# Stage B of a two-layer attention kernel: alternating scale and add on GpSimd, a PSUM copy in the normalisation, and split key buffers

## The chip, the cores and the metric

The kernel is one program on one NeuronCore of a Trainium2 chip. The metric is the device time of one launch in microseconds. The kernel before takes 1666.49 us as the median of three runs (1663.46 to 1671.07). The work is laid out over the engines of the core: TensorE (PE in the profile, with its weight loads shown apart as PEld), VectorE (DVE), ScalarE (ACT), GpSimd (POOL), and SyncE (SP), whose queue issues most of the DMAs.

## The reference

The reference is a two-layer transformer block on 1024 image tokens (`x`) and 256 context tokens (`ctx`), 1024 wide, everything in float32. The even layer projects into two attentions, A (a windowed one) and B, and a gate; the odd layer has two other attentions. The change lies in attention B, the differential attention with 4 heads: each head has two queries and two keys of 64 features and one value of 128.

```python
def _diff_attend(q, k, v, lam):
    s = jnp.einsum('bqhte,bkhte->bhtqk', q, k).astype(jnp.float32) * (q.shape[-1] ** -0.5)
    p = jax.nn.softmax(s, axis=-1)
    a = (p[:, :, 0] - lam * p[:, :, 1]).astype(v.dtype)
    return jnp.einsum('bhqk,bkhe->bqhe', a, v)
...
    yb = _sweep_query_blocks(lambda n, qn: _diff_attend(qn, kb_all, vb_all, lam), qb)
    yb = rmsnorm(yb, b_subln_g) * (1.0 - lam_init)
    y = jnp.concatenate([ya.reshape(B, S, -1), yb.reshape(B, S, -1)], axis=-1) * jax.nn.silu(g)
    x = x + gate * (y @ w_out)
```

The latent queries see 1280 keys (1024 latent and 256 context ones); the context queries see the 256 context keys alone.

## The kernel before

The kernel runs in stages, one after the other: start, e1, A, **B**, outE, then the odd layer (o1, D, M, outO). Numbers are held as a high and a low part, so one product costs two or three matmuls. Stage B is `b_scores`, `b_values`, `b_norm` and a filler, `gates`.

- **Units.** There are 20 units: 4 heads, and in each head five pairs of query blocks of 128, in the order (8,9), which are the context queries, then (0,1), (2,3), (4,5), (6,7). A unit runs its scores, then its values; after unit (8,9), (2,3) and (6,7) a normalisation follows, 12 in all, 8 of four blocks and 4 of two.
- **Scores** (`b_scores`, lines 881 to 932). For each of the two blocks and of the two halves `t`, three chunks of keys are multiplied into PSUM (`sps`, line 909), VectorE moves them to an SBUF tile `sB_t` with the running minimum (line 407), ScalarE takes the exponential (line 917). There are 7 such tiles (`S_BUFS_B`). The keys of a head are one tile `kb` of both halves, and there is one buffer for it (`K_BUFS_B` = 1), so the load for the next head (line 886) can go only when the last score of this head has been multiplied.
- **Mixing.** Half 1 is scaled by `cB` and added to half 0. For the second block VectorE does it in one instruction (line 930); for the first, GpSimd scales five pieces of 256 columns (line 927) and then adds five pieces (line 928, in the helper at line 218).
- **Values** (`b_values`). In steps of two key blocks, four transposes fill one of two PSUM tiles `tps` (`T_PS` = 2, line 958), ScalarE casts the high part `phb` (line 221), VectorE subtracts for the low part `plb` (line 214), and the products go to `pvps` (lines 418 to 420).
- **Normalisation** (`b_norm`). The result is copied out of `pvps` (line 980), transposed into a `tps` tile (line 984), squared and summed by ScalarE out of that tile (line 988); VectorE makes the reciprocal root (lines 990 to 992, 188 to 201) and multiplies out of the same `tps` tile (line 994); the product is transposed back (line 1000) and written out. The `tps` tile is held from line 984 to line 994.
- **Filler.** `gates` projects the gate in eight parts out of the layer's input `hE` (lines 304 to 306), and behind the last of them loads and splits the output weights `woE`, in memory that `hE` has left.

`pipeline` emits these streams in a fixed interleaving; the framework's scheduler then sorts each engine's instructions by its own estimate of when they are ready, and each engine runs its list strictly in that order.

Of the kernel before, what the change touches and what calls it, by code (L numbers as in the profile page):

```python
# [9 lines left out]
F32 = mybir.dt.float32  # L10
F32R = mybir.dt.float32r
BF16 = mybir.dt.bfloat16
I32 = mybir.dt.int32
AF = mybir.ActivationFunctionType
# [17 lines left out]
SM_COND, SM_GE, SM_GO, SM_SUB, SM_SINK, SM_LAM, SM_QG, SM_BE, SM_BO = 0, 16, 24, 32, 33, 41, 297, 300, 316  # L32
SM_N = 332
FILL_A, FILL_B, FILL_D, FILL_M = 5.0, 5.0, 4.3, 5.0
S_BUFS_A, S_BUFS_B, S_BUFS_D, S_BUFS_M, K_BUFS_B, Q_BUFS_B = 11, 7, 12, 6, 1, 3
PH_A, PH_D, PH_M = 3, 3, 4
FILL_O1, HL_BUFS, FILL_E1 = 3.0, 3, 2.3
FILL_Q, FILL_LAT, EMIT_C, RAW_O, RAW_3 = 9.0, 1.5, 1, 1, 2
# [58 lines left out]
def body(nc, tc, I, out, dbg=None):  # L97
# [82 lines left out]
    def f32(ap):  # L180
        return ap.bitcast(F32)
# [694 lines left out]
    with ExitStack() as st:  # L876
        bp = pool(st, "attB", 2, side="left")
        fp = pool(st, "fillB", 2, side="left")
        KB, VBt, OB = {}, {}, {}

        def b_scores(hd, grp, res):
            ctx_q = grp[0] == 8
            q = G if hd == 0 and grp[0] in POOL_Q else SY
            if hd not in KB:
                KB[hd] = bp.tile([P, 2, T], F32R, tag="K", name="kb", bufs=K_BUFS_B)
                q.dma_start(f32(KB[hd]), QK[9 + hd])
            K = KB[hd]
            Q = bp.tile([P, 2, 2, 256], F32R, tag="Q", name="qb", bufs=Q_BUFS_B)
            for half in range(2):
                for t in range(2):  # L890
                    q.dma_start(f32(Q[half * 64:(half + 1) * 64, t]),
                                QK[5 + hd][t * 64:(t + 1) * 64, :, grp[0] * P:grp[0] * P + 256])
            ks = [(S, L)] if ctx_q else list(CHUNKS)
            ncol = sum(n for _, n in ks)
            if grp[0] % 4 == 0:
                OB[hd, "s"] = tiny.tile([P, 4], F32, tag="s0g", name="s0g")
            s0g = OB[hd, "s"]
            Ps = []
            for i in range(2):
                E_ = []  # L900
                ssum = tiny.tile([P, 1], F32, tag="sB", name="sB")
                si = (grp[0] + i) % 4
                for t in range(2):
                    St = bp.tile([P, T], F32, tag="S", name="sB_t", bufs=S_BUFS_B)
                    segs = []
                    for c0, n in ks:
                        ps = s_ps()
                        for hl in range(2):
                            T_.matmul(ps[:, :n], Q[:, t, hl, i * P:(i + 1) * P], K[:, t, c0:c0 + n],  # L909
                                      start=hl == 0, stop=hl == 1)  # L910
                        o0 = c0 - ks[0][0]
                        segs.append((ps[:, :n], St[:, o0:o0 + n], None))
                        if c0 < S:
                            yield
                    m = tiny.tile([P, 3], F32, tag="mB", name="mB")
                    mx = evac(segs, 0.125, BIG, m)
                    A.activation(St[:, :ncol], St[:, :ncol], AF.Exp, bias=mx, scale=-1.0,  # L917
                                 accum_out=s0g[:, si:si + 1] if t == 0 else ssum)
                    E_.append(St)
                    yield  # L920
                cc = tiny.tile([P, 1], F32, tag="cB", name="cB")
                V.reciprocal(cc, ssum)
                V.scalar_tensor_tensor(cc, cc, nlam, s0g[:, si:si + 1], ALU.mult, ALU.mult)  # L923
                if i in POOL_MIX:
                    for c0 in range(0, ncol, 256):
                        e1 = E_[1][:, c0:c0 + 256]
                        G.tensor_scalar(e1, e1, cc, 1.0, ALU.mult, ALU.mult)  # L927
                    tt(G, E_[0][:, :ncol], E_[0][:, :ncol], E_[1][:, :ncol], ALU.add)
                else:
                    V.scalar_tensor_tensor(E_[0][:, :ncol], E_[1][:, :ncol], cc, E_[0][:, :ncol], ALU.mult, ALU.add)  # L930
                Ps.append(E_[0])
            res.append((hd, grp, Ps, s0g))

        def b_values(res, nxt):
# [38 lines left out]
        def b_norm(nxt):  # L973
# [8 lines left out]
            ps = t_ps()  # L982
            for i in range(nq):
                T_.transpose(ps[:, i * P:(i + 1) * P], of[:, i * P:(i + 1) * P], ident)
            ss = tiny.tile([P, 4], F32, tag="ssB", name="ssB")
            junk = bp.tile([P, P], F32, tag="junk", name="junkb", bufs=1)
            for i in range(nq):
                A.activation(junk, ps[:, i * P:(i + 1) * P], AF.Square, accum_out=ss[:, i:i + 1])
            ev = tiny.tile([P, nq], F32, tag=f"evB{nq}", name="evB")
            V.scalar_tensor_tensor(ev, s0g[:, :nq], EPS, s0g[:, :nq], ALU.mult, ALU.mult)  # L990
            V.scalar_tensor_tensor(ev, ss[:, :nq], 1.0 / P, ev, ALU.mult, ALU.add)
            r = rsqrt(ev, nq)
            of2 = bp.tile([P, 512], F32, tag="of", name="of2", bufs=2)
            V.tensor_tensor(of2[:, :w_].rearrange("p (i c) -> p i c", c=P),
                            ps[:, :w_].rearrange("p (i c) -> p i c", c=P),
                            r.unsqueeze(2).to_broadcast([P, nq, P]), ALU.mult)
            yield
            ps = t_ps()
            for i in range(nq):
                T_.transpose(ps[:, i * P:(i + 1) * P], of2[:, i * P:(i + 1) * P], ident)  # L1000
            if b0 == 8:
                A.mul(O[:, S:T], ps[:, :w_], subg)
                A.dma_start(OTE[1][hd][:, S:T], O[:, S:T])
# [614 lines left out]
```

## Time and profile before

| | |
|---|---|
| median of 3 runs | 1666.49 us |
| profiled execution | 1672.37 us, its span 1670.6 us |
| mean granted TensorE clock | 0.989 |
| PE, PEld, DVE, ACT, POOL busy | 95%, 80%, 65%, 47%, 32% of the span |
| stage B | about 478 to 790 us of the span |

The profile shows one execution. A line of a timeline gives the start, the length, the engine, the line of the kernel, what is written and read, and in square brackets how long the engine had been idle before it and what released it. The shares are means over all stages; what a change in stage B is worth has to be read in stage B.

### The profile page before, as it was taken

Reading aid. Unit: us, or ns where it says so; the run is one execution under the profiler, and the core shown is the slowest. Engines: PE = TensorE matmul, PEld = TensorE weight load, DVE = VectorE, ACT = ScalarE, POOL = GpSimd, SP = SyncE. Lnnn points to the kernel's source line nnn. Section 1 sums busy time; section 2 is a strip of 40 time slices with the busy share of each in tenths; the row PEclk is TensorE's granted clock in tenths of the full one; section 3 lists DMA queues with packets and bytes.
Section 4 is the critical chain, followed back from the end, with each engine's and each line's share of the span. In section 5 each row is a group of like instructions: output and inputs, shape, how many; then the busy total and the mean of one; then the engine's idle time right before and its main releaser. Section 6 shows DMA issues by size and latency. Waiting matters only on the chain. (4 is left out here: it accounts for less than half of the span.)

```text
span 1670.6 us, 26785 instructions
## 1 busy us (share of the span) xinstructions
PE 1589.1 (95%) x9266; PEld 1335.8 (80%) x9266; DVE 1088.6 (65%) x2954; ACT 778.1 (47%) x1580; POOL 538.9 (32%) x713
## 2 busy tenths in 40 slices
PE   6998999999998989998899999999999999999997
PEld 3686768888877878887677798989788887898886
DVE  4674129878759887887677446342677756666586
ACT  5443107766646655666333323322466655544421
POOL 0465025554534433333323202120233414322211
PEclk9999999999999999998999999999999999999999
DMA  7447663252253333223745524567865435321372
GB/s 290 174 124 257 220 214 100 83 164 80 73 199 105 107 101 98 89 77 117 214 156 160 181 60 115 179 183 230 214 167 168 129 121 183 114 83 64 103 223 96
DMA packets 147375, 242.99 MB, mean 145 GB/s; under 512 B 10252, under 2 KB 93096, under 8 KB 145064
## 3 DMA queue, kind: packets, MB, share of 16 engines
q1 hardware_dynamic: 142328, 227.91, 44.2%
q10 hardware_dynamic: 4576, 11.54, 1.8%
q8 instruction: 73, 1.20, 0.3%
q0 software_dynamic: 336, 1.84, 0.3%
q14 instruction: 62, 0.51, 0.1%
HBM read 163.50 MB, written 77.74 MB: 144 GB/s over the span
## 5 line engine op out<-in xcount | busy, mean ns | idle before, releaser
L304 PE MATMUL mmps<-hE,whi 128*128 128x512 f32 (+1 forms) x408 | 148.8, 365 | 1.3 <-DVE gg L396 1.3
L218 POOL TENSOR_TENSOR wlo<-wraw,whi 128x256 fp32r<-128x256 f32 x120 | 92.1, 801 | 174.8 <-ACT whi L251 174.7
L306 PE MATMUL mmps<-hE,wlo 128*128 128x512 f32 (+1 forms) x408 | 146.4, 359 | 0.0
L305 PE MATMUL mmps<-hE,whi 128*128 128x512 f32 (+1 forms) x408 | 146.2, 358 | 0.0
L917 ACT ACTIVATE sB_t<-sB_t,mB 128x1280 f32<-128x1280 f32 (+1 forms) x80 | 95.5, 1194 | 60.1 <-DVE sB_t L407 50.5
L909 PE MATMUL sps<-kb,qb 128*128 128x512 f32 (+1 forms) x416 | 107.2, 359 | 6.1 <-DVE sB_t L407 2.5
L927 POOL TENSOR_SCALAR sB_t<-sB_t,cB 128x256 f32<-128x256 f32 x84 | 38.8, 484 | 156.2 <-DVE cB L923 75.9
L1453 POOL TENSOR_SCALAR sM_t<-sM_t,sM 128x1280 f32<-128x1280 f32 x32 | 43.0, 1345 | 137.7 <-DVE sM L1452 106.5
L304 PEld LDWEIGHTS mmps<-hE,whi 128*128 128x128 f32 x408 | 77.5, 190 | 11.4 <-issue 2.1
L407 DVE TENSOR_SCALAR_CACHE_REDUCE sB_t<-sps,mB 128x512 f32<-128x512 f32 (+1 forms) x128 | 78.2, 612 | 12.7 <-PE sps L909 9.7
L306 PEld LDWEIGHTS mmps<-hE,wlo 128*128 128x128 f32 x408 | 77.2, 189 | 9.9 <-issue 0.8
L305 PEld LDWEIGHTS mmps<-hE,whi 128*128 128x128 f32 x408 | 77.3, 189 | 9.3 <-issue 0.8
L909 PEld LDWEIGHTS sps<-kb,qb 128*128 128x128 f32 x416 | 68.7, 189 | 18.5 <-DVE sB_t L407 6.6
L1351 POOL TENSOR_SCALAR sD_t<-sD_t,sD 128x640 f32<-128x640 f32 (+1 forms) x64 | 48.5, 781 | 89.5 <-DVE sD L1348 36.5
L305 PE MATMUL mmps<-hO,whi 128*128 128x512 f32 (+1 forms) x192 | 75.0, 390 | 1.7 <-POOL hO L214 1.6
L218 POOL TENSOR_TENSOR rot<-rot,csE 128x256 f32<-128x256 f32 x52 | 41.3, 817 | 109.0 <-DVE rot L331 105.2
L304 PE MATMUL mmps<-hO,whi 128*128 128x512 f32 (+1 forms) x192 | 75.5, 393 | 0.0
L306 PE MATMUL mmps<-hO,wlo 128*128 128x512 f32 (+1 forms) x192 | 74.5, 388 | 0.0
L784 ACT ACTIVATE sA_t<-sA_t,mA 128x640 f32<-128x640 f32 (+2 forms) x80 | 59.6, 745 | 31.8 <-DVE sA_t L407 29.2
L218 POOL TENSOR_TENSOR yl<-o_in,yh 128x256 fp32r<-128x256 f32 x36 | 32.0, 909 | 125.1 <-ACT yh L869 111.6
L794 POOL TENSOR_SCALAR sA_t<-sA_t,eA 128x640 f32<-128x640 f32 (+2 forms) x80 | 56.2, 726 | 37.9 <-DVE eA L792 13.8
L221 ACT CAST phm<-tps 128x512 fp32r<-128x512 f32 x80 | 45.7, 584 | 48.8 <-PE tps L1480 48.4
(436 smaller groups left out, 5227.2 us busy)
## 6 DMA issues: line engine op xcount, KB each, us to landing
wraw<-w_e SPq DMA_DIRECT2D x26, 512.0 KB
wada<-w_ada_e SPq DMA_DIRECT2D x24, 512.0 KB
wada<-w_ada_o SPq DMA_DIRECT2D x24, 512.0 KB
wraw<-w_o SPq DMA_DIRECT2D x22, 512.0 KB
qb<-qk SPq DMA_DIRECT2D x76, 128.0 KB
qd_t<-qd SPq DMA_DIRECT2D x32, 256.0 KB
qk<-hl SPq DMA_DIRECT2D x10, 512.0 KB
vb<-vh SPq DMA_DIRECT2D x10, 512.0 KB
```

Source lines behind the costliest of these rows:

```text
L218: eng.tensor_tensor(out_[:, cs_], a[:, cs_], b[:, cs_], op)
L221: A.copy(dst_hi, src)
L304: T_.matmul(ps, lh, rh, start=first, stop=False)
L305: T_.matmul(ps, lh, rl, start=False, stop=False)
L306: T_.matmul(ps, ll, rh, start=False, stop=last)
L407: V.tensor_scalar(dst, ps, -scale, prev, ALU.mult, ALU.min, accum_out=acc)
L784: A.activation(St[:, :nl + L], St[:, :nl + L], AF.Exp, bias=mx, scale=-1.0, accum_out=ssum[:, i:i + 1])
L794: G.tensor_scalar(Ps[i][:, :nl + L], Ps[i][:, :nl + L], e[:, i:i + 1], 1.0, ALU.mult, ALU.mult)
L909: T_.matmul(ps[:, :n], Q[:, t, hl, i * P:(i + 1) * P], K[:, t, c0:c0 + n], start=hl == 0, stop=hl == 1)
L917: A.activation(St[:, :ncol], St[:, :ncol], AF.Exp, bias=mx, scale=-1.0, accum_out=s0g[:, si:si + 1] if t == 0 else ssum)
L1351: G.tensor_scalar(Ps[i][:, :w_], Ps[i][:, :w_], ssum[:, i:i + 1], 1.0, ALU.mult, ALU.mult)
L1453: G.tensor_scalar(St, St, ssum, 1.0, ALU.mult, ALU.mult)
```

## The change

Three edits, all in stage B. The keys of a head become two tiles, one for each half, out of three buffers, and the halves of the next head are asked for at the end of units (4,5) and (6,7). GpSimd's mixing goes piece by piece: scale one, add one. The normalisation copies its transposes from PSUM to an SBUF tile `ot` (ScalarE), squares out of it, and multiplies it in place by four instructions of VectorE instead of one.

```diff
-S_BUFS_A, S_BUFS_B, S_BUFS_D, S_BUFS_M, K_BUFS_B, Q_BUFS_B = 11, 7, 12, 6, 1, 3
+S_BUFS_A, S_BUFS_B, S_BUFS_D, S_BUFS_M, K_BUFS_B, Q_BUFS_B = 11, 7, 12, 6, 3, 3
+        def b_keys(hd, t, q):
+            if hd < 4 and (hd, t) not in KB:
+                KB[hd, t] = bp.tile([P, T], F32R, tag="K", name="kb", bufs=K_BUFS_B)
+                q.dma_start(f32(KB[hd, t]), QK[9 + hd][:, t])
...
-            if hd not in KB:
-                KB[hd] = bp.tile([P, 2, T], F32R, tag="K", name="kb", bufs=K_BUFS_B)
-                q.dma_start(f32(KB[hd]), QK[9 + hd])
-            K = KB[hd]
+            for t in range(2):
+                b_keys(hd, t, q)
...
                     for c0 in range(0, ncol, 256):
-                        e1 = E_[1][:, c0:c0 + 256]
+                        e0, e1 = (E_[t][:, c0:c0 + 256] for t in range(2))
                         G.tensor_scalar(e1, e1, cc, 1.0, ALU.mult, ALU.mult)
-                    tt(G, E_[0][:, :ncol], E_[0][:, :ncol], E_[1][:, :ncol], ALU.add)
+                        G.tensor_tensor(e0, e0, e1, ALU.add)
...
+            if grp[0] == 4:
+                b_keys(hd + 1, 0, SY)
+            if grp[0] == 6:
+                b_keys(hd + 1, 1, SY)
...
+            ot = bp.tile([P, 512], F32, tag="of", name="ot", bufs=2)
+            A.copy(ot[:, :w_], ps[:, :w_])
...
-                A.activation(junk, ps[:, i * P:(i + 1) * P], AF.Square, accum_out=ss[:, i:i + 1])
+                A.activation(junk, ot[:, i * P:(i + 1) * P], AF.Square, accum_out=ss[:, i:i + 1])
...
-            of2 = bp.tile([P, 512], F32, tag="of", name="of2", bufs=2)
-            V.tensor_tensor(of2[:, :w_].rearrange("p (i c) -> p i c", c=P),
-                            ps[:, :w_].rearrange("p (i c) -> p i c", c=P),
-                            r.unsqueeze(2).to_broadcast([P, nq, P]), ALU.mult)
+            for i in range(nq):
+                o = ot[:, i * P:(i + 1) * P]
+                V.tensor_scalar(o, o, r[:, i:i + 1], None, ALU.mult)
```

The scheduler sorts the lists anew. They differ from just inside stage B to the first blocks of outE and are the same behind. GpSimd's list of before, at two mixings of head 1 (`sB_t` is a score tile, `cB` the factor, `wlo` a part of the filler's weights):

```order
L218 TENSOR_TENSOR wlo_6224<-wraw_6225,whi_6223 128x256 x4
L927 TENSOR_SCALAR sB_t_6150<-sB_t_6150,cB_6184 128x256 x5
L218 TENSOR_TENSOR sB_t_6098<-sB_t_6098,sB_t_6150 128x256 x5
L927 TENSOR_SCALAR sB_t_6371<-sB_t_6371,cB_6418 128x256 x5
L218 TENSOR_TENSOR sB_t_6294<-sB_t_6294,sB_t_6371 128x256 x5
```

And the same place now, the first of the two mixings:

```order
L218 TENSOR_TENSOR wlo_6238<-wraw_6239,whi_6237 128x256 x4
L930 TENSOR_SCALAR sB_t_6164<-sB_t_6164,cB_6198 128x256 x2
L931 TENSOR_TENSOR sB_t_6108<-sB_t_6108,sB_t_6164 128x256 x2
L930 TENSOR_SCALAR sB_t_6164<-sB_t_6164,cB_6198 128x256 x2
L931 TENSOR_TENSOR sB_t_6108<-sB_t_6108,sB_t_6164 128x256 x2
L930 TENSOR_SCALAR sB_t_6164<-sB_t_6164,cB_6198 128x256
L931 TENSOR_TENSOR sB_t_6108<-sB_t_6108,sB_t_6164 128x256
```

The five adds no longer stand in one row: two scales, two adds, two scales, two adds, one and one.

SP's list of before, where head 0 passes to head 1 (`kb_92` holds the keys of head 1, `qb` are queries, `qk_87` and `qk_88` those of head 0 and 1, `vbt` the values):

```order
L938 DMA vbt<-vb 128x2560
L891 DMA qb<-qk_87 64x2x256 x8
L400 DMA gte_98<-gg 128x1280
L891 DMA qb<-qk_87 64x2x256 x4
L247 DMA wraw<-w_e 128x1024
L891 DMA qb<-qk_87 64x2x256 x4
L891 DMA qb<-qk_88 64x2x256 x8
L247 DMA wraw<-w_e 128x1024
L400 DMA gte_98<-gg 128x1280
L886 DMA kb<-kb_92 128x2560
```

And now:

```order
L945 DMA vbt<-vb 128x2560
L884 DMA kb<-kb_92 128x1280
L894 DMA qb<-qk_87 64x2x256 x8
L400 DMA gte_98<-gg 128x1280
L894 DMA qb<-qk_87 64x2x256 x4
L247 DMA wraw<-w_e 128x1024
L894 DMA qb<-qk_87 64x2x256 x4
L894 DMA qb<-qk_88 64x2x256 x8
L247 DMA wraw<-w_e 128x1024
L400 DMA gte_98<-gg 128x1280
L884 DMA kb<-kb_92 128x1280
```

Half 0 of the next keys has gone up to the start of head 0; half 1 stands where both halves stood.

PE's list of before, at the normalisation of head 1, block group 4 (line 984 transposes into one `tps` tile, line 958 into the other):

```order
L306 MATMUL mmps<-hE_134,wlo 128x256
L984 MATMUL tps<-consts,of 128x128 x4
L418 MATMUL pvps<-phb,vbt 128x256
L419 MATMUL pvps<-phb,vbt 128x256
L958 MATMUL tps<-consts,sB_t 128x128 x4
L420 MATMUL pvps<-plb,vbt 128x256
```

And now (line 991 is the old 984, line 965 the old 958, line 912 a score of head 2):

```order
L306 MATMUL mmps<-hE_134,wlo 128x256
L912 MATMUL sps<-kb,qb 128x256 x2
L991 MATMUL tps<-consts,of 128x128 x4
L965 MATMUL tps<-consts,sB_t 128x128 x4
L418 MATMUL pvps<-phb,vbt 128x256
L419 MATMUL pvps<-phb,vbt 128x256
L420 MATMUL pvps<-plb,vbt 128x256
```

The first score of the next head has come ahead of the normalisation's transposes, and the values' transposes follow these at once.

## Rows read from the trace of the kernel before

**Rows 1.** The page, busy time: engine, us (share of the span), instructions.
```profile
PE 1589.1 (95%) x9266; PEld 1335.8 (80%) x9266; DVE 1088.6 (65%) x2954; ACT 778.1 (47%) x1580; POOL 538.9 (32%) x713
```

**Rows 2.** Windows: stretch, length, busy us by engine, PE clock, DMA share, GB/s.
```profile
478.00:771.00 293.00, 277.09 (x1730) 238.41 (x1729) 248.69 (x800) 177.87 (x355) 112.83 (x188) 0.99 0.29 91
771.00:805.00 34.00, 27.30 (x135) 22.07 (x134) 23.47 (x45) 17.90 (x38) 14.49 (x18) 0.85 0.71 217
611.00:617.00 6.00, 5.30 (x29) 4.95 (x30) 4.72 (x9) 4.29 (x13) 2.20 (x4) 0.72 0.54 196
774.00:781.00 7.00, 6.84 (x36) 6.87 (x36) 3.41 (x7) 3.90 (x8) 1.43 (x2) 0.56 0.51 184
```

**Rows 3.** Timeline of PE in stage B: rows that begin after idle time.
```profile
504.41 1.14 PE L909 MATMUL sps<-kb,qb 128*128 128x256 f32 x4 [1.84 <-DVE sB_t L407]
...
538.95 0.95 PE L909 MATMUL sps<-kb,qb 128*128 128x256 f32 x6 [2.21 <-DMA kb<-kb]
...
611.70 0.63 PE L958 MATMUL tps<-consts,sB_t 128*128 128x128 f32 x4 [2.13 <-DVE plb L214]
...
665.19 0.63 PE L958 MATMUL tps<-consts,sB_t 128*128 128x128 f32 x4 [0.56 <-DVE rsi L188]
...
695.77 0.95 PE L909 MATMUL sps<-kb,qb 128*128 128x256 f32 x6 [1.19 <-issue]
...
742.29 0.63 PE L958 MATMUL tps<-consts,sB_t 128*128 128x128 f32 x4 [1.01 <-DVE rsi L188]
...
774.16 1.09 PE L958 MATMUL tps<-consts,sB_t 128*128 128x128 f32 x4 [2.69 <-DVE plb L214]
```

**Rows 4.** Timeline of SP: loads of the next head's keys, first weight load.
```profile
530.85 0.33 SPq L886 DMA_DIRECT2D kb<-kb  x1
...
688.44 0.33 SPq L886 DMA_DIRECT2D kb<-kb  x1
...
771.28 0.81 SPq L847 DMA_DIRECT2D woraw<-w_out_e  x2
```

**Rows 5.** Timeline of PE and DVE: one normalisation, from transposes to multiplication.
```profile
608.73 0.60 PE L984 MATMUL tps<-consts,of 128*128 128x128 f32 x4
...
620.87 0.69 DVE L994 TENSOR_TENSOR of<-tps,rsy 128x512 f32<-128x512 f32 x1
```

**Rows 6.** Timeline of DVE and POOL at 501 and 607 us.
```profile
501.56 2.18 DVE L991 SCALAR_TENSOR_TENSOR evB<-ssB,evB 128x2 f32<-128x2 f32 x1
...
500.22 3.50 POOL L218 TENSOR_TENSOR sB_t<-sB_t 128x256 f32<-128x256 f32 x5
...
607.97 2.58 DVE L990 SCALAR_TENSOR_TENSOR evB<-s0g 128x4 f32<-128x4 f32 x1
...
607.02 3.50 POOL L218 TENSOR_TENSOR sB_t<-sB_t 128x256 f32<-128x256 f32 x5
```

**Rows 7.** Lines of stage B: count | busy us, mean ns | idle before.
```profile
L218 POOL TENSOR_TENSOR sB_t<-sB_t 128x256 f32<-128x256 f32 x80 | 57.6, 764 | 0.0
L927 POOL TENSOR_SCALAR sB_t<-sB_t,cB 128x256 f32<-128x256 f32 x84 | 38.8, 484 | 156.2 <-DVE cB L923 75.9 <-ACT of L980 28.3 <-PE sps L909 15.0
L980 ACT COPY of<-pvps 128x512 f32<-128x512 f32 (+1 forms) x12 | 6.1, 505 | 3.2 <-PE pvps L420 3.2
L214 POOL TENSOR_TENSOR sB_t<-sB_t 128x256 f32<-128x256 f32 x4 | 2.9, 732 | 0.3
```

**Rows 8.** Single lines: count, ns min/median/max, first and last start, forms.
```profile
L994 DVE TENSOR_TENSOR of<-tps,rsy x12: 414/680/691, 512.5 to 798.1; 128x512 f32<-128x512 f32 x8, 128x256 f32<-128x256 f32 x4
L188 DVE TENSOR_SCALAR rsi<-evB x12: 155/165/703, 504.7 to 792.4; 128x4 int32<-128x4 int32 x8, 128x2 int32<-128x2 int32 x4
L478 DVE TENSOR_SCALAR xt<-xt,rsy x10: 745/747/753, 13.6 to 66.3; 128x1024 f32<-128x1024 f32 x10
```

**Rows 9.** Waits from 470 to 790 us: who waited for whom, us, times, longest.
```profile
DVE sB_t L407 <- POOL sB_t L218: 4.1, 3, 1.5
```

More of the change, by code (lines that the diff above doesn't have):

```diff
@@ L908, in b_scores @@
                         for hl in range(2):
-                            T_.matmul(ps[:, :n], Q[:, t, hl, i * P:(i + 1) * P], K[:, t, c0:c0 + n],
+                            T_.matmul(ps[:, :n], Q[:, t, hl, i * P:(i + 1) * P], KB[hd, t][:, c0:c0 + n],
                                       start=hl == 0, stop=hl == 1)
@@ L999, in b_norm @@
             for i in range(nq):
-                T_.transpose(ps[:, i * P:(i + 1) * P], of2[:, i * P:(i + 1) * P], ident)
+                T_.transpose(ps[:, i * P:(i + 1) * P], ot[:, i * P:(i + 1) * P], ident)
             if b0 == 8:
```

## The prediction

> **What bounds the kernel now.** I read the busy table first, then one table of windows, then the rows in which the bounding engine stood idle, and last the lines of the engines that it waited for. The busy table gives TensorE 95% of the span and nobody else more than 80% [rows 1]; the weight loads overlap it. So the reader is to see that only idle time of TensorE, or time at its lower clock, can be won. In stage B up to the last gate product, 478 to 771 us, TensorE is busy for 277.09 of 293.00 us: 15.9 us are idle [rows 2]. VectorE is busy for 248.69 of them, 85%, ScalarE 61%, GpSimd 39% [rows 2]: VectorE has the least slack, and a row of TensorE that waits mostly waits for it. Six rows before 771 us carry 8.9 of the 15.9 us: 1.84, 2.21, 2.13, 0.56, 1.19 and 1.01 [rows 3]; smaller ones share the other 7.0. Behind 771 us stands one of 2.69 us [rows 3]. Twice the granted clock falls toward the lower of its two levels after such a wait: 0.72 over the 6 us from 611, and 0.56 over the 7 us from 774 [rows 2]; at full clock the same work would have taken 6 x 0.28 = 1.7 us and 7 x 0.44 = 3.1 us less. That is the purse: about 15.9 + 1.7 = 17.6 us before 771 us, and behind it some 5.8 us which are doubtful, since there the weights of the next stage are being loaded: their first load is issued at 771.28 [rows 4], once the gate's input has been read for the last time.
>
> **The key buffers.** The two waits at a change of head are 2.21 us, released by the load of the keys, and 1.19 us, whose releaser the profile doesn't name but which stands at the same place of head 3 [rows 3]. The loads were issued at 530.85 and 688.44 [rows 4] and the scores went on at 538.95 and 695.77 [rows 3]: 8.1 and 7.3 us. Now half 0 is there long before. Half 1 waits until half 0 of the old head has been multiplied for the last time, three chunks earlier than before, and has half the bytes: between 4.1 us (half of 8.1) and 8.1 us if bytes don't set the time. What is left of the 3.4 us lies between nothing and all; I take 1.0 us, since the load both starts earlier and is shorter. Gain 2.4 us. Half 1 stands in SP's list where both halves stood, so the queries behind it are issued no later. The third change of head, from 1 to 2, had no such wait and gives nothing.
>
> **The copy in the normalisation.** It adds 8 copies of 512 columns and 4 of 256 on ScalarE; the same 12 copies exist already and take 6.1 us in all [rows 7]. ScalarE is 61% busy, and it would have stood waiting for the same transposes to square them: I take nothing; without that cover it costs at most 6.1 us. The squares read SBUF instead of PSUM and I take them as equal. In return a transposes' tile that was held from 608.73 to 621.56, 12.8 us [rows 5], is free after about one. While it was held, the values' transposes had one tile, and each step waited for VectorE to have finished the step before. The waits of 0.56 and 1.01 us [rows 3] are of this kind; they go, 1.6 us. So does the 2.69 us at 774.16 [rows 3], where VectorE had put the reciprocal root in front of that low part, with the 3.1 us of clock behind it. But what is late next there is the chain of weight loads that began at 771.28: the gain is between nothing and 5.8 us. I take 2.0, since ScalarE's casts of those weights stood in line behind the same wait. Together 3.6 us.
>
> **Its price on VectorE.** One multiplication took 0.68 us, or 0.41 for two blocks, and never more than 0.69 [rows 8]: 8 x 0.68 + 4 x 0.41 = 7.1 us. Now there are 40 of 128 columns. No row shows that size. Of 1024 columns one takes 0.75 us, of four columns 0.165 [rows 8]; in between that gives 0.24 (an estimate from these two), so 40 x 0.24 = 9.6 us, 2.5 us more. Below, at 0.165, it would be 6.6; above, at the 0.70 that a four-column instruction of this operation took when GpSimd was at work [rows 8], 28 us, 21 more. I take one in four as held up so: 40 x (0.24 + 0.25 x 0.46) = 14.2, or 7 us more on an engine with 44 us to spare. Only what a back transpose on TensorE waits for counts; I take 0.1 us for each of 12 normalisations, 1.2 us.
>
> Why they can be held up is in the rows: the old multiplication read PSUM and its longest was 0.691 us; the tiny `tensor_scalar` on SBUF goes from 0.165 to 0.703 [rows 8]. The Trainium skill (SBUF — State Buffer, Who interferes with whom) says that `tensor_scalar` on SBUF operands can take a port pair that VectorE shares with GpSimd, that whichever comes first keeps it for its whole instruction, and that a VectorE instruction with at most one SBUF input outside those modes doesn't take part. This speaks against the third edit: it moves the multiplication from the side that never waits to the side that does.
>
> **The alternation.** A mixing of GpSimd is 5 scales of 0.48 and 5 adds of 0.76 us by their means, with an overlap between neighbours: five adds run in 3.50 us [rows 6, 7]. Two instructions of VectorE were held by such a run to its very end: 2.18 us from 501.56 (the adds ended at 503.72) and 2.58 us from 607.97 (they ended at 610.52) [rows 6], against 0.16 us undisturbed. TensorE's waits of 1.84 and 2.13 us follow these two, and the clock's 1.7 us the second [rows 2, 3]. GpSimd's list now has the adds in pairs, so if a scale lets VectorE in, the longest hold is two adds, 2 x 0.70 = 1.4 us: about 1 us less in either case. I take 1.0 of the 1.84, 1.2 of the 2.13, and 1.3 of the clock's 1.7, as that follows only a long wait: 3.5 us, with bounds of nothing and 5.7. The mixings themselves grow: four small ones already went from a scale straight to the add that needs it, with 0.3 us of idle time in all [rows 7], 0.08 us each, and the overlap is lost at the five places where the operation changes. I take 0.5 us a mixing. It costs where VectorE waits for a score tile that GpSimd has not left: three times, 4.1 us in all [rows 9]. 3 x 0.5 = 1.5 us; the bounds are 0 and 16 x 0.5 = 8 us. The first piece of a mixing comes earlier now; I take nothing for it.
>
> By that page of the skill the hold lasts for one instruction; the rows of 2.18 and 2.58 us are three adds and more, so here the measurement differs. If the rule held, the order of the pieces would be all the same and the sum would be 3.5 us worse.
>
> **The sum.** 2.4 + 3.6 + 3.5 - 1.2 - 1.5 = 6.8, say 7 us. The profiled execution took 1672.37 us, so 1665.4 for one like it. It lies 5.9 us above the median of the three runs; 1666.49 - 7 gives **1659.5 us**.
>
> **The rivals.**
> - *The waits only move.* VectorE is the slow partner (85%) and gets more work; the lists are sorted anew, and other rows of TensorE find VectorE late. For it speaks that seven of the 15.9 us are small waits that no edit touches; against it that the longest ones have causes that are removed. Only the keys' 2.4 us and little else stay: 1664 us.
> - *The alternation doesn't part the adds.* The pieces follow each other as closely as before, VectorE is held to the end of the whole mixing. For: the adds already followed each other and let it in at one time and not at another. The 3.5 us fall away: 1663 us. I join it with the case above.
> - *Everything goes.* With two tiles for the transposes and keys ahead, the small waits go too, and nearly the whole 17.6 us: 1650 us. Against it is the load on VectorE.
> - *Slower: the multiplications are held up.* One mechanism, in `b_norm`: the four instructions wait one after the other for GpSimd's pieces, 0.70 instead of 0.24 us, VectorE gets 21 us more, and the low parts behind them come late to TensorE. It decides once more than half of the 40 meet GpSimd; GpSimd was busy for 39% of the stage, and its mixing starts in the same units. If half of the 21 us and 6 us of fresh clock loss and score tile waits reach TensorE, against 7 won: 1666.5 + 16 - 7 = 1676 us.
>
> **How the numbers follow.** Chances: the forecast 0.52, with a range of its own from 1655 to 1664; waits that move or stay 0.20; everything goes 0.12; slower 0.16. 0.5%, about what a measurement of this kernel can tell from no change, is 8.3 us. Faster by more than that: 0.12 and half of the forecast's 0.52 (its sum may well come out at 9 or 10), 0.38. Slower by more: the last rival and a little of the second, 0.17. Between: 0.45. The range for 8 in 10 reaches from 1649 to 1672: it leaves out most of the slow case, and holds the rest.
>
> **What would show it.** In the profile after: no row of TensorE that waits for `kb`, or one under 1 us; between the normalisation's transposes and the copy about 1 us, and transposes of values waiting for VectorE less often; no VectorE row of `evB` above 1.5 us, if the alternation parts the adds, and GpSimd's stretches of ten pieces at 6.3 us instead of 5.8; the four multiplications at 0.24 us each, or at 0.7 where GpSimd runs. The idle time of TensorE in the stage should fall from 15.9 to about 10 us. I am wrong if it doesn't fall, if the weights at the end of the stage set the time whatever comes before, or if the new rows wait for VectorE as long as the old ones did.

## The result, and the profile after

The changed kernel takes 1682.05 us as the median of six runs, the kernel before 1667.35 us in runs beside them: the ratio is 1.0084, with a 95% interval from 1.0066 to 1.0102. It is slower by 14 us, where 1659.5 was forecast. One of the six executions took 5459.96 us and stands outside the ratio; the median of the other five is 1681.67. The profiled execution took 1686.15 us (span 1684.4).

The first view is the page's busy table, as in [rows 1].

```profile
PE 1597.4 (95%) x9266; PEld 1342.7 (80%) x9266; DVE 1085.8 (64%) x2982; ACT 782.5 (46%) x1592; POOL 538.1 (32%) x714
```

TensorE does the same 9266 matmuls and is busy for 8.3 us more. The windows say where (columns as in [rows 2]): stage B up to the last gate product, and five stretches of 10 us inside it.

```profile
481.80:789.80 308.00, 286.55 (x1733) 246.07 (x1733) 248.82 (x819) 182.58 (x367) 112.16 (x188) 0.97 0.26 85
510.00:520.00 10.00, 8.74 (x53) 8.17 (x53) 8.56 (x34) 4.60 (x9) 1.02 (x3) 0.83 0.04 13
590.00:600.00 10.00, 7.62 (x31) 5.40 (x30) 6.82 (x25) 2.72 (x4) 5.72 (x10) 0.84 0.18 52
680.00:690.00 10.00, 8.20 (x45) 7.17 (x46) 7.02 (x19) 4.80 (x8) 0.93 (x2) 0.83 0.04 14
710.00:720.00 10.00, 7.66 (x43) 6.69 (x43) 6.04 (x18) 2.92 (x5) 1.14 (x2) 0.83 0.11 32
760.00:770.00 10.00, 6.98 (x33) 5.34 (x32) 6.52 (x20) 2.91 (x6) 5.78 (x10) 0.87 0.05 15
```

The stage takes 308.0 us against 293.0 [rows 2], 15.0 us more. TensorE is idle in it for 21.5 us against 15.9, so 5.5 us are waits. The other 9.5 are slower products: over the stage's windows of 10 us, the part of full clock that was not granted adds up to 10.2 us, against 1.7 before. The stretches shown are the pattern: a wait, and the granted clock at 0.83 to 0.87 around it. The stage began 3.8 us later, behind instructions that stand in the same order in both kernels, and after its end some 5 us came back: the two profiled executions differ by 13.8 us.

The waits of TensorE that answer to [rows 3], of those of 1.5 us and more all but one (its timeline; in square brackets the idle time and what ended it):

```profile
511.26 0.48 PE L304 MATMUL mmps<-hE,whi 128*128 128x256 f32 x1 [1.89 <-DVE gg L396]
...
538.57 1.51 PE L912 MATMUL sps<-kb,qb 128*128 128x256 f32 x6 [2.07 <-DMA kb<-kb]
...
596.60 1.67 PE L912 MATMUL sps<-kb,qb 128*128 128x512 f32 x3 [1.54 <-DVE sB_t L407]
...
681.80 1.01 PE L912 MATMUL sps<-kb,qb 128*128 128x512 f32 x2 [2.13 <-DVE sB_t L407]
...
712.54 0.30 PE L1008 MATMUL tps<-consts,ot 128*128 128x128 f32 x1 [2.34 <-DVE ot L1004]
...
766.65 0.73 PE L912 MATMUL sps<-kb,qb 128*128 128x512 f32 x2 [2.13 <-DVE sB_t L407]
```

Three of the six are scores that wait for VectorE's line 407, which moves a chunk of scores out of PSUM into a score tile. They lie in the stretches at 590, 680 and 760 us, which with the windows just behind them hold 5.1 of the 10.2 us of missing clock. The other three waited for VectorE at the gate, for the keys and for the new multiplications, and the other 5.1 us are around them: the stretches at 510 and 710 us and a fall around 540 us. Before each of the three scores VectorE itself had stood, at the first chunk of a new tile, on the timeline of DVE:

```profile
595.84 0.69 DVE L407 TENSOR_SCALAR_CACHE_REDUCE sB_t<-sps 128x512 f32<-128x512 f32 x1 [1.98 <-POOL sB_t L931]
...
681.05 0.69 DVE L407 TENSOR_SCALAR_CACHE_REDUCE sB_t<-sps 128x512 f32<-128x512 f32 x1 [3.05 <-POOL sB_t L931]
...
765.90 0.69 DVE L407 TENSOR_SCALAR_CACHE_REDUCE sB_t<-sps 128x512 f32<-128x512 f32 x1 [3.05 <-POOL sB_t L931]
```

It waited for GpSimd's last add (line 931) to leave a tile. In all of the stage, the waits give for this pair:

```profile
DVE sB_t L407 <- POOL sB_t L931: 14.5, 7, 3.1
```

That is seven times and 14.5 us, where [rows 9] had three times and 4.1 (4.8 with one small mixing of 0.7 us on line 214). The mixing was hardly slower. The middle one of the three, on POOL's timeline:

```profile
675.14 0.94 POOL L930 TENSOR_SCALAR sB_t<-sB_t,cB 128x256 f32<-128x256 f32 x2 [7.93 <-DVE rst L200]
676.03 1.43 POOL L931 TENSOR_TENSOR sB_t<-sB_t 128x256 f32<-128x256 f32 x2
677.43 0.94 POOL L930 TENSOR_SCALAR sB_t<-sB_t,cB 128x256 f32<-128x256 f32 x2
678.33 1.42 POOL L931 TENSOR_TENSOR sB_t<-sB_t 128x256 f32<-128x256 f32 x2
679.72 0.49 POOL L930 TENSOR_SCALAR sB_t<-sB_t,cB 128x256 f32<-128x256 f32 x1
680.29 0.72 POOL L931 TENSOR_TENSOR sB_t<-sB_t 128x256 f32<-128x256 f32 x1
```

It runs from 675.14 to 681.01, 5.87 us, some 0.1 us longer than the usual mixing before (5.80 us). VectorE had nothing else in front of the blocked instruction from 678.0 on, and everything behind it, the low parts and the next scores, stood too. Now count the score tiles of the stage by the first instruction that fills each, from 0 to 79, the same in every kernel here. The three are numbers 35, 55 and 75. In the kernel before, number 55 had been filled like this:

```profile
672.24 0.69 DVE L407 TENSOR_SCALAR_CACHE_REDUCE sB_t<-sps 128x512 f32<-128x512 f32 x1 [1.64 <-PE tps L958]
```

There it waited for the values' transposes, while GpSimd's mixing ran on to 676.2 without holding it (POOL's timeline, the kernel before):

```profile
670.44 2.31 POOL L927 TENSOR_SCALAR sB_t<-sB_t,cB 128x256 f32<-128x256 f32 x5 [8.72 <-DVE cB L923]
672.70 3.53 POOL L218 TENSOR_TENSOR sB_t<-sB_t 128x256 f32<-128x256 f32 x5
```

The tile had been given another slot, that is, another of the seven buffers. The built programs say so without any time: these are the first instructions of tiles 55 and 75 with the engines that they wait for, in the kernel before and in the kernel after.

```
L407 TENSOR_SCALAR sB_t_7486,mB_7512<-sps_7487 128x512 [waits PE_49]
L407 TENSOR_SCALAR sB_t_8495,mB_8514<-sps_8496 128x512
...
L407 TENSOR_SCALAR sB_t_7514,mB_7540<-sps_7515 128x512 [waits PE_49,Pool_49]
L407 TENSOR_SCALAR sB_t_8535,mB_8554<-sps_8536 128x512 [waits PE_49,Pool_49]
```

Before, neither waits for GpSimd; after, both do. Tile 55 gets the slot that the mixing of tiles 52 and 53 leaves, the one just ahead of it; before, that slot went to tile 57. At head 3 the slot of the mixing of tiles 72 and 73 went to tile 77 before and goes to 75 after. Which of the seven slots a new tile gets is decided when the program is built, along with the order of the instructions.

This is not all of it. Tiles 55 and 75 carry 6.1 of the 14.5 us. The five others, numbers 21, 35, 43, 53 and 61, wait in both programs for the same mixing, and came to 8.4 us after and to 3.5 before. There only the times at which VectorE and GpSimd arrive have moved.

### The profile page after: what moved, and what is told of

Its sections match the earlier page's. It is cut to its first block, busy times and chain, and to the rows that moved or that the text cites. A ratio compares the mean times of both kernels' runs of the same rounds, so it can differ in the third digit from the quotient of the medians.

```text
span 1684.4 us, 26855 instructions
## 1 busy us (share of the span) xinstructions
PE 1597.4 (95%) x9266; PEld 1342.7 (80%) x9266; DVE 1085.8 (64%) x2982; ACT 782.5 (46%) x1592; POOL 538.1 (32%) x714
## 3 DMA queue, kind: packets, MB, share of 16 engines
q0 software_dynamic: 480, 1.84, 0.3%
## 5 line engine op out<-in xcount | busy, mean ns | idle before, releaser
L912 PE MATMUL sps<-kb,qb 128*128 128x512 f32 (+1 forms) x416 | 111.9, 368 | 8.8 <-DVE sB_t L407 6.6
L912 PEld LDWEIGHTS sps<-kb,qb 128*128 128x128 f32 x416 | 71.0, 194 | 21.5 <-DVE sB_t L407 11.0
```

What stands on the lines that cost most here:

```text
L912: T_.matmul(ps[:, :n], Q[:, t, hl, i * P:(i + 1) * P], KB[hd, t][:, c0:c0 + n], start=hl == 0, stop=hl == 1)
```

## The experiments

The theory after reading the two traces: the change re-sorted the work, and the builder then gave some score tiles a slot that GpSimd was still mixing; VectorE stood there, TensorE behind it, and the clock fell. The rivals: the alternation holds the tiles longer; the four multiplications hold VectorE; the copy is dear; the keys held ahead crowd the tiles. Ratios are to the kernel before on the same chip. The fourth column is the length of stage B up to the last gate product, the fifth VectorE's waits in line 407 for GpSimd, both from one profile.

| run | edit to | ratio (95%) | stage B, us | waits, us |
|---|---|---|---|---|
| before | | 1 | 292.9 | 4.8 |
| after | | 1.0084 (1.0066 to 1.0102) | 308.0 | 14.5 |
| 1 keys alone | before | 0.9990 (0.9974 to 1.0006) | 292.6 | 6.3 |
| 2 normalisation alone | before | 1.0068 (1.0049 to 1.0088) | 308.6 | 11.3 |
| 3 alternation alone | before | 0.9977 (0.9962 to 0.9992) | 288.6 | 5.0 |
| 4 eight tiles | after | 1.0010 (0.9995 to 1.0025) | 294.7 | 3.4 |
| 5 copy, one multiplication | before | 1.0072 (1.0051 to 1.0094) | 302.7 | 12.2 |
| 6 four multiplications, no copy | before | 1.0033 (1.0017 to 1.0048) | 295.5 | 9.6 |
| 7 alternation, eight tiles | before | 0.9946 (0.9932 to 0.9961) | 283.9 | 0 |
| 8 keys and alternation | before | 0.9978 (0.9966 to 0.9990) | 289.9 | 9.4 |
| 9 copy, PSUM held | before | 1.0020 (1.0009 to 1.0031) | 296.8 | 9.8 |
| 10 normalisation, eight tiles | before | 0.9989 (0.9975 to 1.0002) | 292.8 | 3.1 |
| 11 eight tiles | before | 0.9961 (0.9945 to 0.9978) | 290.9 | 0 |
| 12 keys, alternation, eight tiles | before | 0.9951 (0.9931 to 0.9970) | 285.9 | 0 |
| 13 own slots, 4 and 3 | after | 0.9971 (0.9957 to 0.9984) | 285.8 | 0 |
| 14 normalisation, slots 4 and 3 | before | 0.9971 (0.9956 to 0.9986) | 288.2 | 0 |
| 15 alternation, slots 4 and 3 | before | 0.9979 (0.9964 to 0.9994) | 286.5 | 0 |
| 16 alternation, slots 5 and 3 | before | 0.9968 (0.9953 to 0.9983) | 286.3 | 1.7 |
| 17 slots 4 and 3 | before | 1.0009 (0.9996 to 1.0022) | 286.9 | 0 |
| 18 slots 5 and 3 | after | 1.0007 (0.9993 to 1.0021) | 292.9 | 1.7 |

**The three parts alone.** Run 1 takes from the change only what concerns the keys:

```diff
+        def b_keys(hd, t, q):
...
+            if grp[0] == 4:
+                b_keys(hd + 1, 0, SY)
```

> Only the key edit, in the kernel before. The theory (late tile): all of the loss is VectorE standing in front of a score tile that GpSimd is still mixing (14.5 us in the kernel after, 4.1 before), because the lists are sorted anew and VectorE reaches that instruction earlier, relative to the mixing. With keys ahead the scores of the next head come without a pause, so if that is what brings VectorE there too early, this part alone shows over 8 us of that wait and +5 to +10 us over the kernel before. The rival (the normalisation is the cause): this part gives its own gain, -2 to -3 us (1664 to 1665), and that wait stays near 4 us.

Measured 1668.54 against 1670.28 us: no loss, and the gain of 1.7 us is not clear of nothing. Run 2 has only the normalisation:

```diff
+            ot = bp.tile([P, 512], F32, tag="of", name="ot", bufs=2)
+            A.copy(ot[:, :w_], ps[:, :w_])
...
+                V.tensor_scalar(o, o, r[:, i:i + 1], None, ALU.mult)
```

> Only the normalisation's copy and its four multiplications per group, in the kernel before. If the normalisation is the cause, +8 to +15 us (1675 to 1682), with VectorE waiting 10 us or more for score tiles that GpSimd mixes, or TensorE's back transposes waiting some 7 us for the multiplications. The rival (the keys or the alternation are the cause): between -4 and +3 us, with the wait of the transposes for a free PSUM tile gone all the same.

1681.62 us, 11.3 more than before, and a stage B of 308.6 us: nearly the whole loss. VectorE waits for GpSimd's tiles 11.3 us, 2.09 of them at tile 35 and 3.37 at tile 55. Run 3 has only the alternation:

```diff
+                        e0, e1 = (E_[t][:, c0:c0 + 256] for t in range(2))
...
+                        G.tensor_tensor(e0, e0, e1, ALU.add)
```

> Only the alternation, in the kernel before; the order of the other engines hardly moves. The theory (late tile through a new order): within 3 us of the kernel before. The rival (the alternation itself: GpSimd leaves its two tiles later and holds up VectorE): +6 us or more, mixings over 6.3 us from start to end against 5.82, and over 10 us of VectorE's wait for tiles that GpSimd mixes.

1667.93 against 1670.28 us, faster by 0.23%. Of the three the normalisation alone loses, and the alternation holds nobody up.

**More tiles.** Run 4 gives the kernel after an eighth tile and takes one of the keys' three half buffers for it.

```diff
-S_BUFS_M, K_BUFS_B, Q_BUFS_B = 11, 7, 12, 6, 3, 3
+S_BUFS_M, K_BUFS_B, Q_BUFS_B = 11, 8, 12, 6, 2, 3
```

> The kernel after with eight score tiles in place of seven; to make room the keys have two half buffers in place of three. The theory (late tile): VectorE no longer stands before a tile in GpSimd's hands; that wait falls from 14.5 to under 5 us and the time from 1682 to about 1668 or below. The rival (multiplications or alternation hold VectorE up directly): the tiles matter little and the time stays within 4 us of 1682.

1671.23 us: the waits fall to 3.4 us, the missing clock from 10.2 to 1.7 us, and the loss is gone, though nothing is gained over the kernel before. The order of the work hardly moved for it: 92 of the 2502 instructions on VectorE's list stand at another place, and none on GpSimd's.

**Which half of the normalisation.** Run 5 is run 2 with one multiplication for all blocks, on the copy. Run 6 is the kernel before, multiplying block by block out of PSUM without a copy.

```diff
+            V.tensor_tensor(ot[:, :w_].rearrange("p (i c) -> p i c", c=P),
...
-                V.tensor_scalar(o, o, r[:, i:i + 1], None, ALU.mult)
```

> The kernel before with the normalisation's copy out of PSUM, but with one multiplication for all blocks, as before, now on the copy. Theory A (the copy is the cause: with the PSUM tile free early the work is put in another order, in which VectorE comes to a score tile that GpSimd is still mixing): most of the loss stays, 1676 to 1684 us, and that wait stays at 10 us or more. Theory B (the four multiplications are the cause: 36 instructions of 0.35 us, before the back transposes): the loss goes, 1664 to 1670 us, and the wait falls to 4 or 5 us.

```diff
-            V.tensor_tensor(of2[:, :w_].rearrange("p (i c) -> p i c", c=P),
...
+                V.tensor_scalar(of2[:, c], ps[:, c], r[:, i:i + 1], None, ALU.mult)
```

> The kernel before, its normalisation still working from PSUM without a copy, but with four multiplications of 128 columns in place of one. Theory A (the copy): within 4 us of the kernel before, since the PSUM tile is held as long as before. Theory B (the four multiplications): most of the loss, 1676 to 1684 us.

The copy alone costs as much as the whole normalisation (12 us), the four multiplications alone half of it (5.5 us). They don't add up to run 2, and neither theory holds by itself. (The multiplications are 40, where the expectation for run 5 says 36.) Both kernels have the waits; run 6 has its longest at tile 75:

```profile
749.39 0.69 DVE L407 TENSOR_SCALAR_CACHE_REDUCE sB_t<-sps 128x512 f32<-128x512 f32 x1 [4.09 <-POOL sB_t L218]
```

Run 9 pays for the copy but leaves the multiplication, and so the PSUM tile, as they were:

```diff
+            A.copy(ot[:, :w_], ps[:, :w_])
...
+                A.activation(junk, ot[:, i * P:(i + 1) * P], AF.Square, accum_out=ss[:, i:i + 1])
```

> The kernel before with the copy on ScalarE added and squared from, while VectorE still multiplies out of PSUM, all blocks at once: the copy is paid, but the PSUM tile is held as long as before. Theory A (the tile's early release brings the order in which VectorE meets a score tile that GpSimd is mixing): within 4 us of the kernel before, 1665 to 1673 us. Theory C (the copy's own time on ScalarE, 12 copies with the squares behind them, makes the chain longer): 1675 us or more, with the PSUM tile held all the same.

3.3 us slower: the copy's own time on ScalarE is at most a small part, and here too tile 75 waits for GpSimd, 3.90 us. All three touches of this function moved slots for the worse: run 5 at tiles 55 and 75, runs 6 and 9 at tile 75 alone.

**Combinations with room.** Run 7 is the alternation with eight tiles, run 11 eight tiles alone, run 10 the normalisation with eight, run 8 the change without its normalisation and run 12 that with eight tiles and two half buffers. The edits are those above.

> The kernel before with the alternation and with eight score tiles in place of seven. If a wait for a score tile is also what bounds the kernel that only alternates (VectorE waited for GpSimd's tiles 5.0 us there, four times), this gives 3 to 6 us more than the alternation alone: 1659 to 1664 us, and the wait is under 2 us. If the scores only wait elsewhere then (for PSUM or the value transposes), it is the same as the alternation alone, 1664 to 1668 us.

> The change without its normalisation part: keys and alternation together. If the parts add up (-1.7 and -3.8 us measured alone), 1664 to 1665 us, the kernel before less 5 or 6 us. If the tile shortage comes back with the keys held ahead, the gain of the alternation is lost: 1668 us or more, with over 8 us of VectorE's wait for GpSimd's tiles.

> The kernel before with the change's normalisation and eight score tiles. If the score tile in GpSimd's hands carries the loss of the normalisation (11 us over the kernel before), it is gone: within 3 us of the kernel before with eight tiles. If the normalisation also costs by itself (back transposes behind four multiplications, 4 to 7 us of waits), 5 us or more over that kernel.

> The kernel before with eight score tiles and nothing else. Its VectorE waited 4.1 us for tiles of GpSimd, and the alternation gained 5 to 6 us more with eight tiles than with seven: 1662 to 1666 us if the eighth tile works by itself; 1668 us or more if it only helps together with the alternation.

> Keys by halves in two half buffers, the alternation and eight score tiles; the old normalisation. If the parts add up: 1659 us, 1 or 2 us below the alternation with eight tiles (1660.7). If two half buffers for the keys leave the wait for them as it was, 1660 to 1662 us, the same as that kernel. A time over 1664 us would say that the keys' order brings a loss of its own.

Run 7 is the fastest by its ratio, 1660.73 us beside 1670.10, with 7.5 us of idle TensorE in the stage; run 12 can't be told from it. Run 11 says that the kernel before gained from an eighth tile too, 0.39%. Run 8 is the change's two good parts: 3.7 us under the kernel before, not the 5 or 6 of a plain sum. It also says that the sum of waits is no price: it has 9.4 us of them, the longest (2.94) at a context tile of 256 columns, but tile 55 waits for the transposes, tile 75 for nobody, and no window of 10 us lost clock. In run 10 the normalisation with eight tiles is still 0.28% above run 11 (0.9989 to 0.9961, each with some 0.15% of uncertainty): with eight slots it costs something, with seven much more. A wider pair says the same: run 4 and run 12 differ by the normalisation alone, both with eight tiles, and stand at 1.0010 and 0.9951. That is some 10 us, and VectorE's waits for GpSimd in run 4 are only 3.4 us. TensorE's own waits for the multiplications are 3.7 us there in the stage, for the old one in run 12 1.7. So a part of what the normalisation costs is not the choice of slots.

**The same seven tiles, with the choice forbidden.** The eighth tile adds room as well as freedom. So in runs 13 to 15 and 17 there are seven tiles, but half 0 and half 1 have slots of their own. A tile of half 0 is left by the values' transposes, one of half 1 by a mixing that is three tiles of its kind ago. In the built program of run 13 tiles 55 and 75 still wait for GpSimd, but for a mixing that is one older: tile 55 for that of tiles 48 and 49, tile 75 for that of 68 and 69.

```diff
-                    St = bp.tile([P, T], F32, tag="S", name="sB_t", bufs=S_BUFS_B)
+                    St = bp.tile([P, T], F32, tag=f"S{t}", name="sB_t", bufs=(4, 3)[t])
```

> The kernel after with its seven score tiles as four slots for the first half (which the values' transposes leave) and three for the second half (which a mixing leaves). If the choice of slot carries the loss: VectorE's wait of 14.5 us for tiles in GpSimd's hands falls to under 6 us and the time to 1668 to 1674 us, 0.5% below the kernel after. If the normalisation is late or dear by itself, or if fixed slots make new waits as long as the old ones: 1678 us or more.

> The kernel before with the change's normalisation and the slots four and three. If the choice of slot carries the loss of 11 us: 1668 to 1673 us, near the same normalisation with eight tiles (1.8 us below the kernel before). If not: 1678 us or more.

> The kernel before with the alternation and the slots four and three; the old normalisation. If fixed slots are worth something only where the choice was bad, this is the alternation alone, 3 to 5 us under the kernel before. If they are as good as an eighth tile: 8 or 9 us under it. If they take freedom away: above it.

Run 13 takes 1665.32 us beside 1671.23, better than any of the expectations: with the same instructions and the same memory for tiles, the kernel after goes from 1.0084 to 0.9971. Their order is not the same, since the lists are sorted anew with it: 484 of the 2502 instructions on VectorE's list stand at another place than in the kernel after. Run 13 shows what the slots and the order that comes with them are worth; the two apart were not tried. There is no wait of line 407 for GpSimd left, and the windows of stage B read:

```profile
477.80:763.60 285.80, 277.57 (x1733) 237.06 (x1732) 251.26 (x818) 182.06 (x367) 117.96 (x187) 1.00 0.28 92
```

285.8 us, with 8.2 idle and the full clock in every window of 10 us. The normalisation alone, run 14, goes from 1.0068 to 0.9971 in the same way. The alternation had no bad slot at tiles 55 and 75 (run 3), and with own slots, run 15, it stays what it was. Then the reference for these, and eight tiles with slots of their own:

> The kernel before with the slots four and three and nothing else. If the change is worth what the prediction's sum says once the slots are fixed (about 7 us), this lies near the kernel before, 1669 to 1674 us, against 1665.3 of the kernel after with the same slots. If the fixed slots are the whole gain and the change is worth nothing, it is at 1664 to 1667 us as well.

> The same with eight slots, five and three. With eight tiles hardly any wait for a slot was left, so fixed slots can only match the alternation with eight tiles: 8 to 10 us under the kernel before. Above that, fixed slots bring waits of their own.

> The kernel after with eight score tiles, five and three, and two half buffers for the keys in place of three to make room. If free slots were the rest of its loss with eight tiles (1671.2 us): 1660 to 1664 us. If two half buffers for the keys or the normalisation's own waits were: 1667 us or more.

Own slots alone are worth nothing (1.0009), though that kernel's one profile shows a stage B 6 us shorter. Behind the last gate product it has a wait of TensorE that is longer than any in stage B of the kernels before and after, on PE's timeline:

```profile
773.10 0.77 PE L958 MATMUL tps<-consts,sB_t 128*128 128x128 f32 x4 [4.58 <-DVE of L994]
```

So run 13 against run 17 is the change with the slots held still: 0.9971 / 1.0009 = 0.9962, some 6.3 us faster, with about 3 us of uncertainty from the two intervals. The profiles don't say where these 6.3 us are: stage B is 285.8 us in run 13 and 286.9 in run 17, and from its start to the odd layer's first product, where the lists are the same again, 435.6 and 437.1. Nor do the parts add up with the same slots: against run 17 the normalisation alone is 0.9962 too and the alternation alone 0.9970, so the whole change is worth no more than its normalisation. Run 16 is 5.3 us under the kernel before and misses the 8 to 10 expected. It is not better than seven own slots by more than the intervals; by its ratio it is worse than run 7, just at the edge of what the two intervals can tell. Run 18 missed: 1670.66 us. Its waits for GpSimd are 1.7 us, but the back transposes wait for the multiplications and the scores for keys that have two half buffers in place of three:

```profile
PE tps L1008 <- DVE ot L1004: 7.2, 6, 2.5
PE sps L912 <- DMA kb<-kb: 4.0, 4, 2.0
```

In run 13 the first of these was 3.3 us and the second did not occur. Why the multiplications come late with eight tiles and less so with seven was not tried further and stays open.

## Why the prediction was wrong, point by point

- *The key buffers* (2.4 us to be won): the mechanism half held. The wait at head 3 is gone, but the one at head 1 is still 2.07 us, where I had left 1.0 for all. The load of half 1 was issued on SP at 531.29 and the scores went on at 538.57: 7.3 us for half the bytes, near the upper end of the bounds of 4.1 and 8.1. Counted from the start of the stage the load was issued 3.4 us earlier than before, but TensorE came to these scores 4.1 us earlier too. Alone it gave 1.7 us, not clear of nothing.
- *The copy* (3.6 us to be won): the PSUM tile is free early, as said, and the values' transposes no longer wait for one. Their line, in stage B, had 8.7 us of idle time before it:

```profile
L958 PE MATMUL tps<-consts,sB_t 128*128 128x128 f32 x336 | 53.0, 279 | 8.7 <-DVE plb L214 5.2 <-DVE rsi L188 1.6 <-DVE sB_t L930 0.7
```

and in the kernel after:

```profile
L965 PE MATMUL tps<-consts,sB_t 128*128 128x128 f32 x328 | 54.2, 285 | 1.5 <-DVE sB_t L933 0.7 <-ACT ob L1013 0.4
```

  So the waits went, 7.2 us of them, and still the part cost 11.3 us alone. That "without that cover it costs at most 6.1 us" was no bound either, for I had bounded the copy by its own duration, and the larger part of the loss came through the slots and the order that the builder chose with it.
- *Its price on VectorE* (7 us more work, 1.2 us on the path): the work was rightly sized, its part on the path was not. The 40 multiplications, first by min, median and max in ns, then by busy us and mean ns:

```profile
L1004 DVE TENSOR_SCALAR ot<-ot,rsy x40: 273/281/770, 515.0 to 817.6; 128x128 f32<-128x128 f32 x40
...
L1004 DVE TENSOR_SCALAR ot<-ot,rsy 128x128 f32<-128x128 f32 x40 | 12.4, 367 | 0.1
```

  A mean of 0.367 us makes them 14.7 us against my 14.2 (12.4 of busy time, since neighbours overlap); undisturbed one takes 0.28, not 0.24, and at most 0.77. Only in the four normalisations at which GpSimd was mixing or adding did they take longer, 12 of the 40, about the one in four that I had taken. But TensorE waited 5.0 us in the stage for them before its back transposes, where it had waited 0.4 for the old one: 4.6 more, not 1.2.
- *The alternation* (3.5 us won, 1.5 paid): right, and the best part. Alone it gave 2.3 us by the medians and 3.8 by the ratio (0.9977) of 2.0 forecast. The holds of 2.18 and 2.58 us [rows 6] are gone; in run 3 the same two lines of VectorE, twelve times each, show min, median and max:

```profile
L990 DVE SCALAR_TENSOR_TENSOR evB<-s0g x12: 132/190/774, 495.8 to 760.7; 128x4 f32<-128x4 f32 x8, 128x2 f32<-128x2 f32 x4
...
L991 DVE SCALAR_TENSOR_TENSOR evB<-ssB,evB x12: 149/156/622, 499.9 to 786.5; 128x4 f32<-128x4 f32 x8, 128x2 f32<-128x2 f32 x4
```

  The longest is 0.77 us, about one add (0.764 by its mean, [rows 7]), less than the 1.4 that I had allowed. TensorE's 1.84 us and 2.13 us [rows 3] became 0.64 and 1.04. A mixing takes 5.93 us instead of 5.80, 0.13 more and not 0.5.
- *The step that failed* stands in that same part: "It costs where VectorE waits for a score tile that GpSimd has not left: three times, 4.1 us in all [rows 9]. 3 x 0.5 = 1.5 us". It took the three meetings of [rows 9] as given and priced only how much longer each would be. That was not so: the edits re-sorted the lists, tiles 55 and 75 got slots out of GpSimd's hands (6.1 us), other tiles met the same mixings for longer, and the meetings rose to seven and 14.5 us. TensorE stood 5.5 us more in the stage, and 8.5 us of lower clock came on top, about half of it around these meetings. The upper bound of 8 us rested on the mixing's length too.
- *The rivals.* "The waits only move" named the thing, lists sorted anew and VectorE late elsewhere, and put it at 1664 us, with a chance of hardly 0.01 to come out clearly slower than before. The slower rival had another mechanism, the multiplications held up by GpSimd's pieces; that occurred (0.77 us against 0.28), to 12 of the 40, and is not what cost most. With the slots held still the change is worth 6.3 us, with about 3 of uncertainty, where 6.8 was forecast. That the totals agree doesn't confirm the sum: its parts don't add up there, the profiles place only 1.5 us, and with eight tiles the normalisation costs instead of gaining. This agreement may be luck.

## What to carry to other kernels

When tiles of different lifetime share one ring of slots, an edit anywhere near can decide whose slot the next tile gets; before pricing waits on such a ring, read in the built program what the first instruction of each tile waits for, before and after, since that shows new meetings without any run. Read which instruction of the other engine it is, and not the engine's name alone: in run 13 the same tiles wait for GpSimd too, one mixing further back, and lose nothing. Whether a meeting is late, only a trace says. If a part that should gain loses, hold the slots still (own slots for each kind of tile) and measure it again. And a wait of 2 to 3 us on the bounding engine can cost more than its length where the clock falls around it: here 5.5 us more of waits came with 8.5 us of slower products.

## What the runs showed of the hardware

- In stage B of the kernel after the granted clock fell at six places (around 510, 540, 590, 680, 710 and 760 us), to between 0.83 and 0.89 as the mean of 10 us, between the two levels of 1.2 and 2.4 GHz. Each fall followed a wait of TensorE of 1.5 to 2.3 us in one piece: around the wait that ended at 681.80 us, windows of 2 us read 1.00 from 680, 0.52 from 682, 0.63 from 684 and 1.00 again from 686. Such a wait doesn't always bring a fall: one of 1.66 us at 626 us left its window at 1.00, and so did those of 1.84 and 2.21 us in the kernel before [rows 3]. In run 13, with no wait of over 1.4 us in the stage, no window was below 1.00.
- An instruction of VectorE that met GpSimd's adds was held for about one add once other operations stood between them (0.77 us at most), and to the end of the run of five when they followed one another (2.58 us, [rows 6]). The Trainium skill (SBUF — State Buffer, Who interferes with whom) says that a VectorE instruction with two SBUF inputs contends with a GpSimd instruction that reads SBUF. The hold by the run of five is longer than any one add; the hold by the alternated adds agrees with one.
- TensorE went on with half a key tile (640 KB) 7.3 us after its load was issued, and with whole ones (1280 KB) 8.1 and 7.3 us after [rows 3, 4]. Half the bytes came hardly sooner here; what else stood in the queue was not looked at.
